# Weight sums of a Strassen product moved from GpSimd beside the projections to VectorE beside the first MLP product

## The chip, the cores and the metric

The kernel runs on one core of a Trainium2 chip. The metric is the device time of one execution in microseconds (us). TensorE (PE) multiplies, VectorE (DVE) and GpSimd (POOL) do elementwise work, ScalarE (ACT) evaluates functions and copies, and SyncE (SP) issues nearly all DMAs in one in-order queue. SBUF is the memory on the chip that the engines read; PSUM holds the products.

## The reference, cut to what matters

One decoder layer on 2048 tokens of width 1024 in float32: RMS norm, one input projection, three mixers (a causal convolution with 31 taps, retention, dilated attention), an output projection with residual, and an MLP with hidden width 4096:

```
h2 = rms_norm(x, norm2_g)
ff = square(relu(h2 @ w_ff1)) @ w_ff2
return x + ff
```

The change concerns sums of blocks of `w_ff2`. They depend on that input alone, so they can be made at any time before the second MLP product uses them.

## The kernel before, in words

Every float32 product is made as three matmuls on rounded high and low halves (`hi*hi + hi*lo + lo*hi`). ACT writes the high half (L634) and DVE subtracts it from the raw value to get the low half (L636).

The stages, in order of time: the projections of the convolution and retention parts, with the retention recurrence and the convolution taps between them (to about 440 us); the projections of the attention part with what is left of the taps (to about 685 us); attention (to about 950 us); the output projection (to about 1168 us); then the MLP for each half H of the tokens (1024 each): the first product (H = 0: 1168 to 1489 us; H = 1: 1788 to about 2108 us) and the second one (H = 0: 1489 to 1788 us; H = 1: from 2108 us).

**The MLP** uses Strassen's scheme with seven block products for eight. In the first product a loop over 16 pairs of hidden blocks (`pair(j)`, L1106) makes seven products of twelve matmuls each. Weight sums S1 to S4 of `w_ff1` are made by POOL (`weight_sums`, L1097). A product's stationary operand comes from `op_a` (L1074): ACT copy and DVE subtraction into one of six buffers (`wcp`). Several products accumulate in the same PSUM bank, and DVE reads the bank between two of them (L1114, L1118, L1121 to L1125), so the later product waits for that read. The results go to the DRAM tiles `hid_d`. The second product (L1193) runs through seven products of 16 steps each, and loads in every step one block of weights and one of activations. Its weights are blocks of `w_ff2` or, in the products S1 to S4, sums of them from the DRAM tiles `w2s_d`; the first of these is the third product.

**The sums of `w_ff2`** are made by `w2_sums(j)` (L175), 16 times: two loads of 512 KB (L179), four POOL additions or subtractions of 128x512 (L183), and two stores of 512 KB (L185). Twelve calls stand in the loop over token tiles of the first projections (L464), four in that of the attention projections (L612). Their tiles come from the pool `stage` with three buffers, which the weights of the projections (L112), the bias bands and the attention operands also use. POOL does other small work of the same stages that others wait for: the reciprocal roots (`rsqrt`, L83), the gate products of the retention (L340, L407) and the low halves for attention (L589, L591).

**The order.** The context is opened with `schedule_with_timeline_sim=True` (L1297): the order of the instructions in each engine's queue is chosen when the program is built, on a simulated timeline, with the program's order as the preference. At run time each queue is strictly in order. `load_acc` (L1160) loads the eight residual tiles `acc` for the second product; it is attached to step 6 of the first product (L1190). The pool `ur` has 24 buffers of 4 KB in each partition; while the first MLP product runs, 20 of them hold its right operands (B11, B21, B22, T2, T3), and the result tile `t12` rotates through the rest.

Of the kernel before, what the change touches and what calls it, by code (L numbers as in the profile page):

```python
# [9 lines left out]
F32 = mybir.dt.float32  # L10
# [3 lines left out]
ALU = mybir.AluOpType  # L14
# [4 lines left out]
P = 128  # L19
# [24 lines left out]
CH = 512  # L44
# [3 lines left out]
def kernel(ctx, tc, x, xT, w_in, g1, g2, conv_w, conv_b, conv_g, ret_g, qk_g,  # L48
                             w_out, w_ff1, w_ff2, rel_bias, ident_c, bands_c, rope_c, decay_c,
                             causal_c, groups_c, sel_c, outT):  # L50
    nc = tc.nc
# [11 lines left out]
    NP = NF // 2  # L63
    hid_d = [[[dram.tile([P, 2, CH], F32, name=f"hid_d{h}_{j}_{n}") for n in range(3)] +
              [dram.tile([P, 1, CH], F32, name=f"hid_d{h}_{j}_3")] for j in range(NP)] for h in range(2)]
    w2s_d = [[dram.tile([P, 2, CH], F32, name=f"w2s_d{j}_{n}") for n in range(2)] for j in range(NP)]
# [23 lines left out]
    stage = ctx.enter_context(tc.tile_pool(name="stage", bufs=3))  # L90
# [71 lines left out]
    def bias_bands(b):  # L162
        bands = stage.tile([33, TW], F32, tag="raw", name="bands")
        nc.sync.dma_start(out=bands[:], in_=bands_c[:, b, :])
        for h0 in range(0, HEADS, 2):
            bt = stage.tile([P, 2, TW], F32, tag="raw", name="bt")
            for u in range(2):
                pb = psA.tile([P, 512], F32, tag="c", name="pb", bufs=1)
                nc.tensor.matmul(pb[:, :TW], rb[:, h0 + u:h0 + u + 1].to_broadcast([33, P]), bands[:],
                                 start=True, stop=True)  # L170
                nc.scalar.activation(out=bt[:, u, :], in_=pb[:, :TW], func=AF.Copy)
            for u in range(2):
                nc.sync.dma_start(out=band_d[(h0 + u) * 3 + b].rearrange("(q w) -> q w", w=TW), in_=bt[:, u, :])

    def w2_sums(j):  # L175
        ra, rb = [stage.tile([P, 2, 512], F32, tag="raw", name=n) for n in ("w2sa", "w2sb")]
        for u, t in enumerate((ra, rb)):
            f = 2 * j + u
            nc.sync.dma_start(out=t[:], in_=w_ff2[f * P:(f + 1) * P, :].rearrange("p (h c) -> p h c", h=2))  # L179
        for out, a, b, op in ((rb[:, 1], ra[:, 1], rb[:, 1], ALU.add), (ra[:, 1], ra[:, 0], ra[:, 1], ALU.subtract),  # L180
                              (ra[:, 0], rb[:, 1], ra[:, 0], ALU.subtract),
                              (rb[:, 0], rb[:, 0], ra[:, 0], ALU.subtract)):
            nc.gpsimd.tensor_tensor(out=out, in0=a, in1=b, op=op)  # L183
        for u, t in enumerate((ra, rb)):
            nc.sync.dma_start(out=w2s_d[j][u][:], in_=t[:])  # L185


    x_first = [load_x(0, 4)]
# [2 lines left out]
    def prefetch(i, n=KT):  # L191
        hq[i] = split_x(x_first.pop(0) if x_first else load_x(i), n)
# [13 lines left out]
    rb = cv1.tile([33, HEADS], F32, name="rb")  # L206
# [227 lines left out]
    def go(g, taps=0):  # L434
        next(g, None)
        some_conv(taps)
# [14 lines left out]
    for i in range(2, NT - 2):  # L451
        c, r, b = conv_of[i], ret_of[i], ret_of[i - 1]
        go(c, 1)
        go(b, 1)
        if i == 2:
            go(ret_of[0])
        go(r, 1)
        go(b, 1)
        go(c, 1)
        prefetch(i + 1)  # L460
        go(r, 1)
        if 4 <= i < 7:
            bias_bands(i - 4)
        w2_sums(i - 2)  # L464
        go(r, 0)
        go(b, 0)
        go(r, 0)
# [107 lines left out]
    def load_tables(p):  # L575
        return [band_table(p, b, b < 2) for b in range(3)]

    def build(p, c, wait=0):
        cs = slice(c * CH, (c + 1) * CH)
        for h in range(2):  # L580
            raw = stage.tile([P, 2, CH], F32, tag="raw", name="qkraw")
            for u in range(2):
                nc.sync.dma_start(out=raw[u * 64:(u + 1) * 64], in_=qkT_d[p][c][h * 64:(h + 1) * 64])

            def parts(h=h, raw=raw):
                with tc.issue_after(last[0].ins):
                    nc.vector.tensor_copy(out=qs[h][:, cs], in_=raw[:, 0, :])
                    nc.vector.tensor_copy(out=khi[h][:, cs], in_=raw[:, 1, :])
                nc.gpsimd.tensor_tensor(out=qs[h][64:P, cs], in0=raw[64:P, 0, :],  # L589
                                        in1=qs[h][64:P, cs].bitcast(F32), op=ALU.subtract)  # L590
                nc.gpsimd.tensor_tensor(out=klo[h][:, cs], in0=raw[:, 1, :], in1=khi[h][:, cs].bitcast(F32),  # L591
                                        op=ALU.subtract)

            if wait:
                todo.append([wait, parts])
            else:
                parts()

    go(att_of[0])
    for i in range(2, NT):  # L600
        go(att_of[i], 1)
        go(att_of[i - 1])
        if i + 1 < NT:
            prefetch(i + 1)
        go(att_of[i], 1)
        go(att_of[i])
        if i % 4 == 1 and i > 4:
            build(0, i // 4 - 1)
        if i == 8:
            tabs = load_tables(0)  # L610
        if i % 2 == 0 and i <= 8:
            w2_sums(NP - 5 + i // 2)  # L612
    go(att_of[NT - 1])
    some_conv(100)
    second.close()
# [278 lines left out]
    def bank(name):  # L894
        turn[0] += 1
        tag = ("mm", "s", "pt", "o", "mm", "s", "pt", "c")[turn[0] % 8]
        return psA.tile([P, CH], F32, tag=tag, name=name, bufs=1 if tag in "oc" else 2)
# [27 lines left out]
    ur = ctx.enter_context(tc.tile_pool(name="ur", bufs=UNITS, side="right", reuse_waits="tile"))  # L925
# [19 lines left out]
    def tt(eng, out, a, b, op):  # L945
        eng.tensor_tensor(out=out, in0=a, in1=b, op=op)  # L946
# [53 lines left out]
    def right_ops(H, names):  # L1000
        for name, h, c in (("T3", 0, 1), ("T1", 0, 0), ("T4", 4, 0), ("B22", 4, 1)):
            if name in names:
                for kp in range(4):
                    op_b(name, kp, x1[H, kp + h][:, c, :])
# [59 lines left out]
                               5: [lambda: right_ops(0, ("T3", "T1"))]})  # L1064
    right_ops(0, ("T4", "B22"))

    for H in range(2):

        def load_w1(f):
# [36 lines left out]
        def pair(j, begun=None, loaded=None):  # L1106
            if not loaded:
                ra, rb = load_w1(2 * j), load_w1(2 * j + 1)
                loaded = ra, rb, weight_sums(ra, rb)
            ra, rb, (s12, s34) = loaded  # L1110
            dt, et, xb = begun or first_half(ra)
            yb = bank("psy")
            product(yb[:], op_a("S2", s12[:, 1, :]), "T2", True, True)
            tt(nc.vector, dt[:, 1, :], et[:, 0, :], yb[:], ALU.add)  # L1114
            if not begun:
                second_half(ra, dt, xb)
            product(yb[:], op_a("S3", s34[:, 0, :]), "T3", False, True)
            tt(nc.vector, et[:, 1, :], et[:, 0, :], yb[:], ALU.add)  # L1118
            zb = bank("psz")
            product(zb[:], op_a("S1", s12[:, 0, :]), "T1", True, True)  # L1120
            tt(nc.vector, et[:, 1, :], et[:, 1, :], zb[:], ALU.add)  # L1121
            product(yb[:], op_a("A22", rb[:, 1, :]), "T4", False, True)
            tt(nc.vector, et[:, 0, :], et[:, 0, :], yb[:], ALU.add)
            product(zb[:], op_a("S4", s34[:, 1, :]), "B22", False, True)
            tt(nc.vector, dt[:, 1, :], dt[:, 1, :], zb[:], ALU.add)  # L1125
            for t in (et[:], dt[:, 1, :]):
                nc.scalar.activation(out=t, in_=t, func=AF.Relu)
            for t in (et, dt):
                nc.scalar.activation(out=t[:], in_=t[:], func=AF.Square)
            t12 = unit4(ur, "u", "t12", F32)  # L1130
            nc.sync.dma_start(out=hid_d[H][j][1][:], in_=et[:])
            tt(nc.vector, t12[:, 0, :], dt[:, 1, :], dt[:, 0, :], ALU.subtract)
            tt(nc.vector, t12[:, 1, :], et[:, 1, :], t12[:, 0, :], ALU.subtract)
            tt(nc.vector, dt[:, 1, :], et[:, 1, :], dt[:, 1, :], ALU.subtract)
            nc.sync.dma_start(out=hid_d[H][j][0][:], in_=dt[:])
            nc.sync.dma_start(out=hid_d[H][j][2][:], in_=t12[:])
            tt(nc.vector, et[:, 0, :], et[:, 0, :], t12[:, 1, :], ALU.subtract)
            nc.sync.dma_start(out=hid_d[H][j][3][:], in_=et[:, 0:1, :])

        begun = []  # L1140
        ra, rb = load_w1(0), load_w1(1)
        loaded = ra, rb, weight_sums(ra, rb)
        begun.append(first_half(ra))
        for j in range(1, FIRST):
# [3 lines left out]
            ra = rj  # L1148
# [34 lines left out]
        def left_next():  # L1183
            for kp in range(4):
                for name, k in (("B11", kp), ("B21", kp + 4)):
                    op_b(name, kp, x1[1, k][:, 0, :])

        steps = {} if H else {(3, 8): load_next, (4, 2): lambda: normalise(1, 0), (4, 8): lambda: normalise(1, 1),
                              (5, 6): left_next, **{(6, 9 + kp): lambda kp=kp: act_sums(1, kp) for kp in range(4)}}
        steps[0, 6] = load_acc  # L1190
        sb = banks(("mm", "mm", "s", "s"))
        zb = banks(("pt", "pt", "o", "c"))
        for n, (an, bn, chain, dh, c, done) in enumerate((  # L1193
# [7 lines left out]
            for j in range(NP):  # L1201
                pool, tag = (stage, "raw") if n == 0 and j < 7 else (ur, "u")
                raw = pool.tile([P, 2, CH], F32, tag=tag, name="ffraw")
# [9 lines left out]
            for d in range(4):  # L1213
                t = acc[dh + d][:, c, :]
# [86 lines left out]
```

## Time and profile before

| what | value |
|---|---|
| median of 3 runs | 2416.18 us (2404.49 to 2425.15) |
| the profiled execution, its own time | 2412.23 us |
| its span, first to last instruction | 2410.1 us |
| PE busy | 2340.6 us (97%) |
| DVE busy | 1529.0 us (63%) |
| ACT busy | 1100.7 us (46%) |
| POOL busy | 592.4 us (25%) |
| mean granted TensorE clock | 0.981 |

Busy shares are means over stages. PE's time lies in the stretches where it idles or where its granted clock is below 1, and both are in the stages before the MLP. A wait is put down to the event that came last; the line of a helper (L636, L946) stands for all its uses, which the tile names tell apart.

### The profile page before, as it was taken

Reading aid. Unit: us, or ns where it says so; the run is one execution under the profiler, and the core shown is the slowest. Engines: PE = TensorE matmul, PEld = TensorE weight load, DVE = VectorE, ACT = ScalarE, POOL = GpSimd, SP = SyncE. Lnnn points to the kernel's source line nnn. Section 1 sums busy time; section 2 is a strip of 40 time slices with the busy share of each in tenths; the row PEclk is TensorE's granted clock in tenths of the full one; section 3 lists DMA queues with packets and bytes.
Section 4 is the critical chain, followed back from the end, with each engine's and each line's share of the span. In section 5 each row is a group of like instructions: output and inputs, shape, how many; then the busy total and the mean of one; then the engine's idle time right before and its main releaser. Section 6 shows DMA issues by size and latency. Waiting matters only on the chain.

```text
span 2410.1 us, 33394 instructions
## 1 busy us (share of the span) xinstructions
PE 2340.6 (97%) x11678; PEld 1957.3 (81%) x11678; DVE 1529.0 (63%) x2944; ACT 1100.7 (46%) x2309; POOL 592.4 (25%) x427
## 2 busy tenths in 40 slices
PE   7999999998999999899999999999999999999999
PEld 7878788898987777687888888888887888888887
DVE  5496979685348676568565555676576555565554
ACT  6443223533357667444444444545444444454442
POOL 1332661534213242334422330000022322000000
PEclk9999999999989899999999999999999999999999
DMA  7532552644245353855344447974624444698640
GB/s 239 167 116 91 164 181 60 187 122 141 77 99 109 80 115 87 288 184 178 109 166 153 145 144 273 379 260 123 205 101 144 144 145 146 213 381 286 194 146 35
DMA packets 256532, 396.45 MB, mean 164 GB/s; under 512 B 47485, under 2 KB 136684, under 8 KB 256364
## 3 DMA queue, kind: packets, MB, share of 16 engines
q1 hardware_dynamic: 253804, 385.93, 49.1%
q0 software_dynamic: 2560, 8.39, 0.9%
q8 instruction: 92, 1.51, 0.3%
q14 instruction: 76, 0.62, 0.1%
HBM read 280.30 MB, written 113.93 MB: 164 GB/s over the span
## 4 chain that ended last, share of the span: by engine, by line
PE 76%; DVE 11%; DMA 7%; POOL 2%; issue 2%; ACT 1%; SPq 1%; ACTq 0%; POOLq 0%; DVEq 0%
PE pso L934 25%; PE psy L934 11%; PE ps L160 10%; PE psx L934 7%; PE psz L934 7%; DVE acc L231 4%; PE psc L934 4%; PE po L729 2%; PE pt L708 2%; PE sp L682 2%; PE sp L683 2%; DMA xn<-x 2%; DMA ml_d<-ml 1%; DMA qkraw<-qkT_d 1%; DMA woraw<-w_out 1%
## 5 line engine op out<-in xcount | busy, mean ns | idle before, releaser
L934 PE MATMUL pso<-hid,w 128*128 128x512 f32 x2688 | 610.2, 389 | 0.0
L934 PEld LDWEIGHTS pso<-hid,w 128*128 128x128 f32 x2688 | 504.5, 188 | 105.1 <-ACT hid L634 0.2
L160 PE MATMUL ps<-whi,hh 128*128 128x384 f32 (+1 forms) x896 | 316.4, 354 | 14.8 <-ACT whi L119 9.5
L160 PE MATMUL ps<-whi,hl 128*128 128x384 f32 (+1 forms) x896 | 316.6, 353 | 0.5 <-DVE hl L152 0.5
L160 PE MATMUL ps<-wlo,hh 128*128 128x384 f32 (+1 forms) x896 | 314.4, 351 | 0.0
L634 ACT ACTIVATE w<-ffraw 128x512 fp32r<-128x512 f32 x224 | 141.5, 632 | 310.0 <-PE pso L934 273.9
L636 DVE TENSOR_TENSOR w<-ffraw,w 128x512 fp32r<-128x512 f32 x224 | 155.9, 696 | 196.6 <-ACT w L634 195.7
L946 POOL TENSOR_TENSOR s<-w1raw 128x512 f32<-128x512 f32 x64 | 85.2, 1351 | 712.8 <-PE pso L934 322.2
L934 PE MATMUL psy<-T,S 128*128 128x512 f32 x768 | 194.4, 395 | 0.0
L160 PEld LDWEIGHTS ps<-whi,hh 128*128 128x128 f32 x896 | 170.9, 191 | 28.4 <-ACT whi L119 9.5
L231 DVE SCALAR_TENSOR_TENSOR acc<-cbuf,cwt,acc 128x512 f32<-128x512 f32 x240 | 192.1, 849 | 0.2
L934 PE MATMUL psx<-B,A 128*128 128x512 f32 x768 | 189.7, 395 | 0.0
L160 PEld LDWEIGHTS ps<-whi,hl 128*128 128x128 f32 x896 | 171.1, 191 | 10.1 <-issue 2.7
L160 PEld LDWEIGHTS ps<-wlo,hh 128*128 128x128 f32 x896 | 171.1, 191 | 9.5 <-issue 2.7
L934 PEld LDWEIGHTS psx<-B,A 128*128 128x128 f32 x768 | 143.9, 187 | 35.1
L934 PEld LDWEIGHTS psy<-T,S 128*128 128x128 f32 x768 | 143.8, 187 | 34.7
L934 PE MATMUL psc<-mix,wohi 128*128 128x512 f32 x512 | 165.3, 403 | 6.1 <-ACT wohi L658 3.9
L636 DVE TENSOR_TENSOR hid<-ffraw,hid 128x512 fp32r<-128x512 f32 x224 | 152.7, 685 | 6.2 <-ACT hid L634 4.9
L636 DVE TENSOR_TENSOR S<-s,S 128x512 fp32r<-128x512 f32 x128 | 112.5, 883 | 58.2 <-ACT S L634 57.7
L693 ACT ACTIVATE lt<-lt,ml 128x256 f32<-128x256 f32 (+1 forms) x288 | 129.2, 452 | 28.9 <-DVE ml L690 28.2
L634 ACT ACTIVATE hid<-ffraw 128x512 fp32r<-128x512 f32 x224 | 137.2, 618 | 6.7 <-DMA ffraw<-hid_d 6.4
L634 ACT ACTIVATE A<-w1raw 128x512 fp32r<-128x512 f32 x96 | 60.1, 628 | 170.6 <-PE psy L934 126.7
(196 smaller groups left out, 3997.2 us busy)
## 6 DMA issues: line engine op xcount, KB each, us to landing
ffraw<-hid_d SPq DMA_DIRECT2D x224, 256.0 KB, 5.2
w1raw<-w_ff SPq DMA_DIRECT2D x66, 512.0 KB, 3.6
ffraw<-w2s_d SPq DMA_DIRECT2D x128, 256.0 KB, 4.0
ffraw<-w_ff SPq DMA_DIRECT2D x96, 256.0 KB, 5.3
woraw<-w_out SPq DMA_DIRECT2D x33, 512.0 KB, 4.3
hid_d<-hidB SPq DMA_DIRECT2D x32, 512.0 KB, 3.6
hid_d<-t SPq DMA_DIRECT2D x32, 512.0 KB, 2.6
hid_d<-hidA SPq DMA_DIRECT2D x32, 512.0 KB, 3.3
```

What stands on the lines that cost most here:

```text
L160: nc.tensor.matmul(ps, a[:, k, :], b[k][:], start=(k == 0 and m == 0), stop=(k == KT - 1 and m == 2))
L231: nc.vector.scalar_tensor_tensor(out=accs[j], in0=src, scalar=cwt[:, j, w:w + 1], in1=accs[j], op0=ALU.mult, op1=ALU.add)
L634: nc.scalar.activation(out=u[:, 0, :], in_=raw, func=AF.Copy)
L636: sub.tensor_tensor(out=u[:, 1, :], in0=raw, in1=u[:, 0, :].bitcast(F32), op=ALU.subtract)
L682: nc.tensor.matmul(sp[:, c0:c0 + n], qs[h][:, qsl], khi[h][:, ksl], start=True, stop=False)
L683: nc.tensor.matmul(sp[:, c0:c0 + n], qs[h][:, qsl], klo[h][:, ksl], start=False, stop=True)
L693: last_exp[0] = nc.scalar.activation(out=lt[:, :n], in_=lt[:, :n], func=AF.Exp, scale=-1.0, bias=mls[u][:, h:h + 1], accum_out=mls[u][:, 2 ...
L708: nc.tensor.transpose(pts[u][:, q * P:(q + 1) * P], lts[h, u][:, c * P:(c + 1) * P], ident[:])
L729: nc.tensor.matmul(po[h * 64:(h + 1) * 64, u0 * P:(u0 + n) * P], vt[:, kv, h * 64:(h + 1) * 64], mv, start=(one or i == 0), stop=(one or i ...
L934: nc.tensor.matmul(ps, w[a], act[b], start=(first and m == 0), stop=(last and m == 2), skip_group_check=more)
L946: eng.tensor_tensor(out=out, in0=a, in1=b, op=op)
```

## The change

`w2_sums` moves into the MLP: it is called from `pair(j)` in the first half (H = 0), after the DVE read of the bank that follows product S3. The calls are spread over j = 1 to 13, one sum each, and two at j = 4, 8 and 12. Its tiles come from `ur`, and the four operations run on DVE. The calls in both projection loops are gone. `load_acc` goes from step 6 to step 9 of the first of the seven products, in both halves.

```
-        w2_sums(i - 2)
...
-        if i % 2 == 0 and i <= 8:
-            w2_sums(NP - 5 + i // 2)
...
+    def w2_sums(j):
+        ra, rb = [ur.tile([P, 2, CH], F32, tag="u", name=n) for n in ("w2sa", "w2sb")]
+        for u, t in enumerate((ra, rb)):
+            f = 2 * j + u
+            nc.sync.dma_start(out=t[:], in_=w_ff2[f * P:(f + 1) * P, :].rearrange("p (h c) -> p h c", h=2))
+        for out, a, b, op in ((rb[:, 1], ra[:, 1], rb[:, 1], ALU.add), (ra[:, 1], ra[:, 0], ra[:, 1], ALU.subtract),
+                              (ra[:, 0], rb[:, 1], ra[:, 0], ALU.subtract),
+                              (rb[:, 0], rb[:, 0], ra[:, 0], ALU.subtract)):
+            tt(nc.vector, out, a, b, op)
+        for u, t in enumerate((ra, rb)):
+            nc.sync.dma_start(out=w2s_d[j][u][:], in_=t[:])
...
             tt(nc.vector, et[:, 1, :], et[:, 0, :], yb[:], ALU.add)
+            if H == 0 and 0 < j < 14:
+                for n in range(j - 1 + (j > 4) + (j > 8) + (j > 12), j + (j >= 4) + (j >= 8) + (j >= 12)):
+                    w2_sums(n)
...
-        steps[0, 6] = load_acc
+        steps[0, 9] = load_acc
```

## Rows read from the trace of the kernel before

**Rows 1.** Windows: length, busy PE, PEld, DVE, ACT, POOL (instructions), PEclk, DMA share, GB/s.

```profile
60.00:80.00 20.00, 18.57 (x113) 16.06 (x112) 10.78 (x30) 5.25 (x11) 11.63 (x12) 0.86 0.53 171
...
240.00:280.00 40.00, 36.90 (x214) 31.61 (x213) 36.60 (x59) 10.37 (x27) 21.81 (x11) 0.99 0.50 163
280.00:320.00 40.00, 35.55 (x169) 30.21 (x168) 33.71 (x49) 9.47 (x24) 27.98 (x17) 0.84 0.50 165
...
360.00:400.00 40.00, 38.33 (x220) 32.94 (x220) 37.20 (x77) 9.76 (x25) 8.05 (x6) 1.00 0.10 29
...
520.00:560.00 40.00, 33.54 (x186) 33.22 (x185) 35.15 (x42) 10.86 (x19) 23.31 (x14) 0.91 0.59 170
...
1300.00:1400.00 100.00, 100.00 (x432) 80.74 (x431) 57.88 (x82) 45.21 (x67) 27.64 (x20) 1.00 0.43 154
...
1489.00:1550.00 61.00, 61.00 (x270) 50.33 (x269) 38.91 (x61) 33.57 (x56) 0.00 (x0) 1.00 1.03 386
```

**Rows 2.** Windows of line L183 (the sums) alone: POOL busy, clock, DMA.

```profile
240.00:360.00 120.00, 50.30 (x32) 0.94 0.52 173
...
sum 485.00, POOL 97.66; mean POOL 19.53
```

**Rows 3.** Waits in the first 700 us: who waited for whom, us, times, longest.

```profile
PE rpo L379 <- DVE rsm L365: 4.5, 2, 3.7
PE ps L160 <- ACT rv L329: 3.0, 1, 3.0
PE ptq L536 <- DVE raw L526: 10.1, 4, 6.5
ACT rsq L395 <- DVE st L390: 33.0, 10, 12.3
DVE qs L587 <- DMA qkraw<-qkT_d: 13.5, 4, 4.6
POOL w2sb L183 <- DMA w2sb<-w_ff: 34.3, 9, 7.0
SPq L185 <- POOL w2sa L183: 45.4, 14, 6.7
```

**Rows 4.** DVE's convolution taps (L231), by group, from 240, 480 and 526 us.

```profile
L231 DVE SCALAR_TENSOR_TENSOR acc<-cbuf,cwt,acc 128x512 f32<-128x512 f32 x46 | 40.7, 934 | 0.0
...
L231 DVE SCALAR_TENSOR_TENSOR acc<-cbuf,cwt,acc 128x512 f32<-128x512 f32 x38 | 26.7, 745 | 0.1
...
L231 DVE SCALAR_TENSOR_TENSOR acc<-cbuf,cwt,acc 128x512 f32<-128x512 f32 x22 | 23.0, 1078 | 0.1
```

**Rows 5.** Groups of the whole run: DVE on two SBUF inputs in the MLP.

```profile
L946 DVE TENSOR_TENSOR t<-hidA 128x512 f32<-128x512 f32 x32 | 22.2, 692 | 13.7 <-ACT hidA L1129 13.6
```

**Rows 6.** Timeline of one pair, DVE: start, length, instruction, idle before it.

```profile
1302.34 0.69 DVE L946 TENSOR_TENSOR hidB<-hidB,psy 128x512 f32<-128x512 f32 x1 [1.44 <-PE psy L934]
1303.01 0.69 DVE L636 TENSOR_TENSOR S<-s,S 128x512 fp32r<-128x512 f32 x1
...
1306.29 1.69 DVE L636 TENSOR_TENSOR S<-s,S 128x512 fp32r<-128x512 f32 x1 [2.00 <-ACT S L634]
...
1321.85 0.69 DVE L946 TENSOR_TENSOR hidB<-hidB,psy 128x512 f32<-128x512 f32 x1 [1.45 <-PE psy L934]
```

**Rows 7.** Timeline of the same pair: PE, then POOL.

```profile
1307.51 0.63 PE L934 MATMUL psy<-T,A 128*128 128x512 f32 x2
...
1304.89 2.54 POOL L946 TENSOR_TENSOR s<-w1raw 128x512 f32<-128x512 f32 x2 [14.02 <-DMA w1raw<-w_ff]
```

**Rows 8.** SP's waits in the first MLP product of the first half.

```profile
SPq L1071 <- DVE A L636: 147.6, 27, 10.5
```

**Rows 9.** The tile acc from 1460 to 1560 us: durations min/median/max, first to last.

```profile
L1163 SPq DMA_DIRECT2D acc<-x_d x8: 320/320/400, 1473.3 to 1488.0; - x8
L946 DVE TENSOR_TENSOR acc<-acc,pso x4: 680/680/689, 1526.7 to 1529.7; 128x512 f32<-128x512 f32 x4
...
DMA to landing us min/median/max: 5.8/7.5/8.8
```

More of the change, by code (lines that the diff above doesn't have):

```diff
@@ L173, in bias_bands @@
                 nc.sync.dma_start(out=band_d[(h0 + u) * 3 + b].rearrange("(q w) -> q w", w=TW), in_=bt[:, u, :])
[L175 to L185, printed above, removed]
     x_first = [load_x(0, 4)]
```

## The prediction

> **What bounds the kernel now.** I read the windows by stage first, to find where TensorE loses time at all. In the first product of the MLP's first half, where the sums are to go, PE is busy 100.00 of 100 us at clock 1.00, and likewise in the second product behind it [rows 1]. Nothing can be won there; the question is only whether the new work makes PE wait. Before the attention PE does lose time. I count a window's loss as its idle time plus the clock's shortfall times its length (below 1.00 part of the window ran at 1.2 instead of 2.4 GHz). From 60 to 80 us that is 1.43 + 0.14 x 20 = 4.2 us; from 240 to 280, 3.10 + 0.4 = 3.5; from 280 to 320, 4.45 + 0.16 x 40 = 10.9; from 520 to 560, 6.46 + 0.09 x 40 = 10.1 [rows 1]. Together 28.7 us.
>
> Next, line L183 alone, to see whether the sums stand there. They take 97.66 us of POOL, and 50.30 of these lie between 240 and 360 us [rows 2]. Then the waits, to see who held PE: mostly DVE results that came late (3.7 us for `rsm`, 6.5 us for `raw`), or an ACT copy, itself behind an ACT square that waited 12.3 us for DVE [rows 3]. Last, why DVE is late: its queue is nearly full there (36.60, 33.71 and 35.15 of 40 us [rows 1]), and a convolution tap takes 745 ns where no sum runs, 934 ns from 240 us and 1078 ns from 526 us [rows 4]. So the sums on POOL slow DVE, DVE is late, PE stops and then runs for a while at the lower clock.
>
> **The parts, costed.**
> *Removed, 64 POOL operations beside the projections.* What they take from DVE, by the taps alone: 46 x (934 - 745) ns = 8.7 us in 240 to 320, and 22 x (1078 - 745) ns = 7.3 us in 526 to 562 [rows 4]. Against that stand PE's longest waits of 3.0 and 3.7 us in the one stretch and 6.5 in the other [rows 3], so most of them should close, and the low clock behind them. I don't take all. POOL's operations for the attention operands and the reciprocal roots stay and slow DVE too, and DVE's wait of up to 4.6 us for `qkraw` [rows 3] has nothing to do with the sums. Of the 14.4 us between 240 and 320 I take 10, of the 10.1 behind 520 I take 6. Both are choices nearer to the upper end (all of it) than to the lower one (nothing, if another late result takes the place). From 60 to 80 us one sum is in the way early: POOL waits for its loads up to 7.0 us [rows 3], and the roots queue behind. I take 3 of the 4.2 us. Sum 19 us; bounds 0 and 28.7.
>
> *Removed, 64 DMAs and their places in SP's queue.* SP waited 45.4 us in L185 for POOL [rows 3], with loads of `x` and weights behind it. This is part of the same stalls, so it is not counted again; what hides it is PE's work queued ahead.
>
> *Added, 64 DVE operations in the first product.* The nearest row is DVE on two SBUF tiles of the same shape, 692 ns [rows 5]: 64 x 0.692 = 44 us. A pair takes 1321.85 - 1302.34 = 19.5 us [rows 6], and DVE is idle 42.12 of 100 us [rows 1], so 8.2 us a pair, against 4 x 0.692 = 2.8 us in ten pairs and 5.5 in three. On throughput it fits and costs nothing; if DVE were full, all 44 us would be paid.
>
> What can cost is order. DVE reads the bank after product S3 at 1302.34 to 1303.03 [rows 6], and the next product into that bank starts at 1307.51 [rows 7], a margin of 4.5 us. Four sums in front of such a read use 2.8 of it; a wait for their loads may use more. Behind that wait DVE's low halves and the other reads stand in queue, and PE waits for them. I take 2 us for the whole stage: two spare operand tiles per sum can be loaded well before DVE reaches it, because four of the 24 `ur` buffers are free of operands. Bounds 0 and the slow rival's price.
>
> Beside POOL a DVE operation of this kind takes 1.69 instead of 0.69 us [rows 6], one each pair. The Trainium skill (SBUF — State Buffer, "Who interferes with whom") says that a DVE instruction with two SBUF inputs and a GpSimd instruction that reads SBUF exclude each other, and that the one issued second blocks. The row agrees, and the rule speaks against the new place as well as the old one, since POOL makes the other weight sums there. Were each of the 64 to meet one such block of 1.0 us (the row's difference), they would take 108 us in place of 44; DVE's idle time in 13 pairs is 13 x 8.2 = 107 us. So by the rule at its worst DVE would be just full in these pairs, and at its best nothing changes in the sum.
>
> *Added, 64 DMAs in the first product.* A sum moves 4 x 0.52 MB = 2.1 MB in a pair, 108 GB/s on top of 154 [rows 1], twice that in the three double pairs: 262 and 370 GB/s. The second product runs at 386 GB/s with PE never idle [rows 1], so bandwidth is free. In SP's queue they are 4 x 0.32 us a pair (the length of an issue [rows 9]), where SP stands 147.6 us waiting at the `w_ff1` loads anyway [rows 8]. A store that waits for DVE holds these loads back. POOL starts at the moment its load lands, after 14.02 us of idleness [rows 7], so such a delay passes on to the sums S1 to S4, but their operands are made several products ahead. I put 0, bounded by the slow rival.
>
> *Moved, `load_acc` by three steps.* The eight loads start between 1473.3 and 1488.0 us and land after at most 8.8; the first use is at 1526.7 [rows 9]. The margin is 1526.7 - 1496.8 = 29.9 us. From the first load to the first use are 53 us, and no more than the product's sixteen steps lie in them, so three steps are about 10 us. It costs nothing, in both halves.
>
> **Sum:** 19 - 2 = 17 us less than the profiled execution's 2412.2 gives 2395. The median of the runs is 4 us above that execution, so on the median's scale it is 2399; I say 2398.
>
> **Rivals.**
> *All stalls close.* The 28.7 us go, and also the idle 1.67 us from 360 to 400, where DVE is busy 37.20 of 40 [rows 1]: 30 us, 2386 on the median's scale, or a little less if more of the low clock goes. For it: in each stretch the slowed DVE time is larger than PE's longest wait. Against: the same taps must still be done by DVE there, and the queue order is chosen anew, so that every earlier end may be spent on another wait.
>
> *The stalls are filled again.* Without the sums the next late thing holds PE: DVE's taps or `qkraw`. Then 0 to 8 us are won, 2408 to 2416. For it: DVE is at 84 to 92% of these windows, and without the taps' slowing still at (36.60 + 33.71 - 8.7) / 80 = 77% and (35.15 - 7.3) / 40 = 70% [rows 1, 4]. Against: PE was idle there only in short pieces, which the slowed operations cover.
>
> *Slower: DVE waits for the sums' loads.* On POOL the first operation waited for its load in 9 of 16 sums, 34.3 us in all, 3.8 on average [rows 3]. The same on DVE in front of a bank read passes the margin: 2.8 + 3.8 - 4.5 = 2.1 us of PE idleness each, 19 us for nine; with 7.0 us in all sixteen, 16 x 5.3 = 85 us. Taking 40, less the 17 won, the time is about 2439. It decides as soon as a wait exceeds 1.7 us at the wrong place. For it: the call stands right behind a bank read, and one queue orders all of DVE. Against: the loads need nothing but a free buffer, and in the old place three `stage` buffers were shared with the projection weights.
>
> **How the numbers follow.** Forecast 45%, all stalls close 22%, filled again 20%, slower 13%. About 1% (24 us) is what a measurement can tell from no change, so faster means below 2392. The forecast's own bounds (2385 to 2408) reach below that with about 9 of its 45%, which with the 22% makes faster 0.31 in all. Slower by over 1% (above 2440) is more than half of the slow rival, 0.08; the rest, 0.61, is no change. The range leaves out the far ends of the two outer cases: 2379 to 2425.
>
> **What would show it.** PE's idle time and clock loss between 240 and 320 us and between 520 and 560 us fall to some 4 us each; taps there take near 745 ns; the wait of PE for `raw` shrinks. In the first product of the first half PE stays busy in every microsecond at 19.5 us a pair, and DVE rises from 58 to about 72%. The forecast is wrong if PE waits for DVE in that product, or if the projections end no earlier than now because new waits stand where the old ones were.

## The result, and the profile after

The changed kernel takes 2384.44 us (median of 4 runs, 2382.88 to 2392.27) against 2419.41 for the kernel before (4 runs). The ratio is 0.9865, with a 95% interval of 0.9835 to 0.9896: faster by 1.0 to 1.7%. The medians are 35 us apart. The profiled executions differ by 2412.23 - 2384.19 = 28.0 us, and the time is accounted on those two. They are one execution each: over all series the kernel before ran from 2404 to 2433 us, so a few microseconds of such an account are not firm.

Where the 28 us come from is seen from the first and last start of one stage's matmuls. This is the view by tile of the changed kernel (duration minimum, median and maximum in ns, then first and last start in us): the last transposes of the attention projections, the output projection, and the first MLP product of the first half alone.

```profile
L523 PE MATMUL ptq<-ident,raw x96: 270/272/330, 453.6 to 656.8; 128*128 128x128 f32 x96
...
L919 PE MATMUL psc<-mix,wohi x512: 387/393/793, 922.4 to 1139.0; 128*128 128x512 f32 x171
...
L919 PE MATMUL psx<-B,A x384: 392/396/476, 1139.4 to 1443.0; 128*128 128x512 f32 x192
```

The same starts in the kernel before are 473.8 and 683.9, 948.4, and 1168.5 to 1471.9. So the projections end 683.9 - 656.8 = 27.1 us earlier. Attention takes 265.6 in place of 264.5 us, and the output projection 217.0 in place of 220.1. The first MLP product, which now holds the sums, spans 303.6 us in place of 303.4. The last PE instruction starts 27.5 us earlier, so the projections hold nearly all of it.

The windows of the changed kernel that answer to [rows 1] (columns as there; what comes after the earlier stalls has moved, so the line from 500 to 540 answers to 520 to 560):

```profile
60.00:80.00 20.00, 20.00 (x135) 17.61 (x134) 9.07 (x37) 9.33 (x24) 5.52 (x7) 1.00 0.49 144
80.00:100.00 20.00, 17.79 (x91) 14.47 (x89) 6.01 (x19) 10.21 (x25) 5.68 (x7) 1.00 0.52 159
240.00:280.00 40.00, 40.00 (x221) 35.24 (x220) 35.60 (x68) 11.71 (x28) 14.02 (x6) 1.00 0.21 59
280.00:320.00 40.00, 40.00 (x265) 34.59 (x264) 24.14 (x57) 13.97 (x38) 6.64 (x5) 1.00 0.13 40
500.00:540.00 40.00, 38.76 (x231) 38.40 (x230) 30.77 (x50) 14.26 (x25) 13.67 (x7) 1.00 0.44 111
1240.00:1340.00 100.00, 100.00 (x433) 80.76 (x431) 77.83 (x110) 46.61 (x67) 31.21 (x22) 1.00 0.79 288
1340.00:1440.00 100.00, 100.00 (x432) 80.73 (x431) 72.16 (x103) 48.16 (x70) 27.96 (x19) 1.00 0.72 258
```

PE neither idles nor loses clock between 240 and 320 us, where it had lost 14.4; of the 10.1 us lost from 520 to 560, 1.2 are left. A smaller loss appears at 80 to 100 us (2.2 us idle). In the first MLP product PE is busy in all of 200 us at clock 1.00, while DVE rises from 58 to 72 and 78%, and the DMA rate to 258 and 288 GB/s.

The taps of the changed kernel, by line, in two stretches that begin at 240 and at 526 us (busy us and mean ns of one behind the bar), answering to [rows 3, 4]:

```profile
L219 DVE SCALAR_TENSOR_TENSOR acc<-cbuf,cwt,acc 128x512 f32<-128x512 f32 x46 | 34.4, 793 | 0.0
...
L219 DVE SCALAR_TENSOR_TENSOR acc<-cbuf,cwt,acc 128x512 f32<-128x512 f32 x6 | 4.5, 748 | 0.1
```

And its waits: PE's for `raw`, then DVE's for the loads of the sums in their new place (who waited for whom, us, times, longest).

```profile
PE ptq L523 <- DVE raw L513: 4.2, 3, 2.4
...
DVE w2sb L931 <- DMA w2sb<-w_ff: 12.2, 8, 2.2
```

The last row is the slow rival's event: DVE does wait for the loads, in 8 of 16 sums and up to 2.2 us. No PE wait stands against it in that stage. The timeline shows why: here is DVE in one such pair.

```profile
1228.94 0.68 DVE L931 TENSOR_TENSOR hidB<-hidB,t 128x512 f32<-128x512 f32 x1
1231.61 0.69 DVE L931 TENSOR_TENSOR w2sb<-w2sa,w2sb 128x512 f32<-128x512 f32 x1 [1.99 <-DMA w2sb<-w_ff]
1232.22 0.69 DVE L621 TENSOR_TENSOR S<-s,S 128x512 fp32r<-128x512 f32 x1
1232.82 0.69 DVE L931 TENSOR_TENSOR w2sa<-w2sa 128x512 f32<-128x512 f32 x1
1233.54 0.69 DVE L931 TENSOR_TENSOR w2sa<-w2sb,w2sa 128x512 f32<-128x512 f32 x1
1234.27 0.69 DVE L931 TENSOR_TENSOR w2sb<-w2sb,w2sa 128x512 f32<-128x512 f32 x1
1234.88 0.68 DVE L931 TENSOR_TENSOR hidB<-hidB,psy 128x512 f32<-128x512 f32 x1
```

The sum stands ahead of a bank read, at 1234.88. Its wait of 1.99 us falls there too, one other operation (L621) stands among its four, and the read still comes in time for PE.

### The profile page after: what moved, and what is told of

Same layout as the page of the kernel before. It is cut to its first block, busy times and chain, and to the rows that moved or that the text cites. A ratio compares the mean times of both kernels' runs of the same rounds, so it can differ in the third digit from the quotient of the medians.

```text
span 2382.4 us, 33367 instructions
## 1 busy us (share of the span) xinstructions
PE 2328.6 (98%) x11678; PEld 1948.2 (82%) x11678; DVE 1522.4 (64%) x3008; ACT 1101.2 (46%) x2309; POOL 502.1 (21%) x363
## 4 chain that ended last, share of the span: by engine, by line
PE 86%; DMA 6%; DVE 4%; ACT 2%; issue 1%; POOL 1%; SPq 1%; ACTq 0%; DVEq 0%; POOLq 0%
PE pso L919 26%; PE ps L160 16%; PE psy L919 11%; PE psx L919 8%; PE psz L919 7%; PE psc L919 6%; DMA xn<-x 2%; PE po L714 2%; PE pt L693 2%; PE sp L667 2%; PE sp L668 2%; PE rsp L352 1%; DMA qkraw<-qkT_d 1%; DMA ml_d<-ml 1%; PE rpo L367 1%
## 5 line engine op out<-in xcount | busy, mean ns | idle before, releaser
L621 DVE TENSOR_TENSOR w<-ffraw,w 128x512 fp32r<-128x512 f32 x224 | 156.0, 697 | 198.7 <-ACT w L619 197.9
L931 POOL TENSOR_TENSOR s<-w1raw 128x512 f32<-128x512 f32 x64 | 90.1, 1428 | 710.3 <-PE pso L919 320.2
L219 DVE SCALAR_TENSOR_TENSOR acc<-cbuf,cwt,acc 128x512 f32<-128x512 f32 x240 | 175.6, 778 | 0.2
L621 DVE TENSOR_TENSOR hid<-ffraw,hid 128x512 fp32r<-128x512 f32 x224 | 152.9, 686 | 8.0 <-ACT hid L619 7.9
L619 ACT ACTIVATE hid<-ffraw 128x512 fp32r<-128x512 f32 x224 | 137.1, 617 | 16.6 <-DMA ffraw<-hid_d 14.4
L621 DVE TENSOR_TENSOR S<-s,S 128x512 fp32r<-128x512 f32 x128 | 107.0, 839 | 43.6 <-ACT S L619 42.9
```

Of the source, the lines that this page charges most:

```text
L219: nc.vector.scalar_tensor_tensor(out=accs[j], in0=src, scalar=cwt[:, j, w:w + 1], in1=accs[j], op0=ALU.mult, op1=ALU.add)
L619: nc.scalar.activation(out=u[:, 0, :], in_=raw, func=AF.Copy)
L621: sub.tensor_tensor(out=u[:, 1, :], in0=raw, in1=u[:, 0, :].bitcast(F32), op=ALU.subtract)
```

## The experiments

Two theories stood at the start. Theory 1, that of the prediction: POOL's operations slow DVE, DVE is late, PE stops. Theory 2: the transfers, with their places in SP's queue and in the three `stage` buffers, are what is late. "Projections end" below is the last start of the `ptq` matmuls, by the same view as above: 683.9 before, 656.8 after. The changed kernel and its five variants (e1, e2, e6, e8, e13) end the projections between 651.6 and 656.8 us, so differences under some 5 us are not read. Each such end is that of one profiled execution; the ratios are over all runs, and all are to the kernel before. The changed kernel's gain is 0.0135 of the time before, and "kept" below is the part of it that a variant does not win.

**e1: no sums at all.** From the changed kernel:

```
-            if H == 0 and 0 < j < 14:
-                ...
...
-            if name in ("A11", "A12", "A22"):
+            if name in ("A11", "A12", "A22") or name[0] == "S":
```

> The changed kernel with the sums left out altogether; the second MLP product reads plain blocks of w_ff2 in their place, in the same number and size (so the result is not the layer's). If the sums are hidden in the first MLP product, as forecast, this is no faster than the changed kernel: 2382 to 2386 us, and PE's gaps stay. If the sums there still cost DVE waits that reach PE, it is 5 to 20 us faster than the changed kernel (2365 to 2380).

2389.59 us, ratio 0.9849 (0.9829 to 0.987); the profiled execution spans 2382.3 us against 2382.4. The median is above the 2382 to 2386 expected, but so is that of the kernel before in the same series (2426.1 us), and the ratio is that of the changed kernel. The sums cost nothing that can be measured in their new place, and the gain is what their removal from the projections is worth.

**e4: the transfers alone beside the projections.** From the kernel before (the loop around the operation goes too):

```
...
-            nc.gpsimd.tensor_tensor(out=out, in0=a, in1=b, op=op)
```

> The kernel before without the 64 POOL operations; the 64 transfers stay beside the projections and store plain weights (so the result is not the layer's). Theory 1, POOL operations slow DVE and hold up POOL's queue: nearly the whole gain comes, 2384 to 2394 us, and the taps fall to about 750 ns. Theory 2, the transfers and their places in SP's queue and the three stage buffers are what is late: no more than a third comes, 2405 to 2416.

2392.24 us, ratio 0.9854 (0.9828 to 0.9879); projections end 655.6. All of the gain, with all 64 transfers still there. The taps fall to 780 ns from 40 to 565 us, not quite to the 750 expected. Between 240 and 320 us PE loses nothing, though the DMA engines are busier than in the kernel before:

```profile
240.00:280.00 40.00, 40.00 (x227) 36.01 (x226) 35.04 (x68) 11.14 (x27) 13.65 (x6) 1.00 0.95 317
280.00:320.00 40.00, 40.00 (x264) 34.62 (x263) 22.64 (x55) 14.20 (x39) 6.43 (x5) 1.00 0.52 182
```

Theory 2 falls: without the POOL operations the transfers cost nothing that can be measured. The run does not tell the operations' length from their waiting for loads, since both are gone.

**e5: the POOL operations alone.** From the kernel before:

```
...
-            nc.gpsimd.tensor_tensor(out=out, in0=a, in1=b, op=op)
...
+        for _ in range(4):
+            nc.gpsimd.tensor_tensor(out=scr[:], in0=scr[:], in1=scr[:], op=ALU.subtract)
```

> The kernel before without the 64 transfers; the POOL operations stay, on a scratch tile that is filled once, and the second product reads plain blocks of w_ff2 (so the result is not the layer's). Theory 1: DVE is still slowed, little is won, 2402 to 2416 us. Theory 2: 2384 to 2396. If both this and the run with transfers only are near 2385, it is the coupling of the two (POOL's queue waiting for a load) that costs.

2404.82 us, ratio 0.9909 (0.9888 to 0.9931); projections end 670.7. Not what was asked: with nothing to wait for, the planner put all 64 between 1.3 and 134.7 us, ahead of the stretches in question. A third of the loss is kept all the same: from 0 to 140 us, where the operations now stand, PE loses 12 us more than in the changed kernel (idle time and clock shortfall). e11 repeats it nearer to the old place.

**e2: the sums on POOL, in the new place.** From the changed kernel:

```
-            tt(nc.vector, out, a, b, op)
+            tt(nc.gpsimd, out, a, b, op)
```

> The changed kernel with the four operations of each sum on POOL, in the new place. If place alone matters, the same time as the changed kernel, 2382 to 2390 us: POOL is busy about 88 of 321 us there and gets about 90 more. If the engine matters (POOL's queue waits for loads in front of the weight sums S1 to S4 of w_ff1, or DVE is slowed too much), 2395 us or more, with PE waiting for ACT or DVE in the first MLP product.

2385.28 us, ratio 0.9838 (0.9808 to 0.9868). POOL's queue waits for the loads even longer than it did beside the projections, and PE waits for nobody in that stage:

```profile
POOL w2sb L931 <- DMA w2sb<-w_ff: 62.9, 9, 13.4
```

So in the new place the choice of engine makes no difference that can be measured; the place is enough.

**e3: the sums on DVE, in the old place.** From the kernel before:

```
-            nc.gpsimd.tensor_tensor(out=out, in0=a, in1=b, op=op)
+            nc.vector.tensor_tensor(out=out, in0=a, in1=b, op=op)
```

> The kernel before with the four operations of each sum on DVE, still beside the projections. If POOL as the engine was the fault, most of the gain comes, below 0.990. If the place is the fault, because DVE's queue is nearly full there (33 to 37 of 40 us) and now gets 44 us of work and the waits for the loads, nothing is won or it is slower: 0.998 to 1.012, with PE waiting for DVE.

2390.13 us, ratio 0.9892 (0.985 to 0.9934); projections end 668.4. The first branch came, "POOL as the engine was the fault", and my expectation for a full DVE was wrong: with 44 us more work on the busiest helper engine the projections still end 15.5 us earlier, of 27.1 with the sums gone from there; by the ratios four fifths of the gain come, and the two intervals overlap. So in the old place the move from POOL to DVE alone wins most of it. DVE's waits for the loads are short:

```profile
DVE w2sb L183 <- DMA w2sb<-w_ff: 10.7, 6, 3.8
```

A full DVE queue is thus not the fault by itself. That left two shares within the POOL operations: their length, shared with DVE, and what they wait for at the head of POOL's queue.

**e9: short POOL operations, all waits kept.** From the kernel before:

```
-            nc.gpsimd.tensor_tensor(out=out, in0=a, in1=b, op=op)
+            nc.gpsimd.tensor_tensor(out=out[:, 0:8], in0=a[:, 0:8], in1=b[:, 0:8], op=op)
```

> The kernel before with the 64 POOL operations cut to 8 of their 512 columns; loads, stores and waits stay (so the sums are incomplete and the result is not the layer's). The run with transfers only won the whole 1.5%, so the cost is in the POOL operations. Theory 1a, their length (DVE shares with them, and POOL's small operations stand behind them): nearly all of the gain again, 0.985 to 0.988 of the time before. Theory 1b, POOL's queue waits for the loads in front of the roots: about half of it or less, 0.992 to 1.000.

2414.92 us, ratio 0.9986 (0.9964 to 1.0009); projections end 678.4 in the profiled execution, the fastest of ten (2405.96 us). Nearly nothing is won, although the taps are as fast as after (777 ns from 40 to 565 us, 778 in the changed kernel, 849 in the kernel before). PE now waits for POOL: first PE's wait, then POOL's timeline at that place.

```profile
PE ptr L411 <- POOL ro L407: 19.7, 2, 14.2
```

```profile
281.34 0.20 POOL L183 TENSOR_TENSOR w2sb<-w2sa,w2sb 128x8 f32<-128x8 f32 x1 [4.85 <-DMA mix_d<-rm]
...
288.53 0.20 POOL L183 TENSOR_TENSOR w2sb<-w2sa,w2sb 128x8 f32<-128x8 f32 x1 [6.15 <-DMA w2sb<-w_ff]
...
289.53 1.32 POOL L83 TENSOR_TENSOR rrr<-rss,power 128x6 f32<-128x6 f32 x1
295.79 0.56 POOL L183 TENSOR_TENSOR w2sb<-w2sa,w2sb 128x8 f32<-128x8 f32 x1 [4.95 <-DMA w2sb<-w_ff]
...
299.75 1.44 POOL L407 TENSOR_TENSOR ro<-ro,rg 128x384 f32<-128x384 f32 x1
```

Three sums stand in POOL's queue ahead of `ro` and wait 4.85, 6.15 and 4.95 us for transfers (the profile puts the first wait down to a transfer to `mix_d`). The retention result `ro`, which PE needs, comes behind the last of them, and PE stands for 14.2 us.

**e12: no stores.** From the kernel before:

```
-        for u, t in enumerate((ra, rb)):
-            nc.sync.dma_start(out=w2s_d[j][u][:], in_=t[:])
...
```

> The kernel before without the 32 stores of the sums; loads and POOL operations stay (the second product reads plain blocks, so the result is not the layer's). A stage buffer is then free 2 to 3 us earlier and SP no longer stands in L185 for POOL. If the chain store, free buffer, load is what holds POOL's queue, a good part of the gain comes, 0.988 to 0.994, and POOL's waits for the loads fall below 20 us. If the POOL operations cost by themselves, 0.996 to 1.000.

2416.9 us, ratio 0.9976 (0.9957 to 0.9995); projections end 688.3, later than before. The waits that the profile puts down to `w2sb` loads did fall (14.2 us in 6), but POOL's idle time in front of the sums as a whole did not (80.8 us against 72.7 before), and PE waited 16.3 us for `ro`, longest 10.7. The stores are not a necessary link: SP's next loads now wait for the buffer that POOL frees, 42.3 us in 4 waits from 200 to 320 us, and POOL's queue is held up without the stores as well.

**e11: full POOL operations in place, no transfers.** From the kernel before (the input is the low halves that the step has just made):

```
-    def w2_sums(j):
...
+    def w2_sums(j, h):
...
+            nc.gpsimd.tensor_tensor(out=scr[:], in0=h[:, 4 * (k % 2):4 * (k % 2) + 4, :] ..., in1=scr[:], op=ALU.subtract)
```

> The kernel before with the 64 POOL operations kept at full size beside the projections, each reading the low halves of the token tile that its step prepares, but without the 64 transfers (the second product reads plain blocks of w_ff2, so the result is not the layer's). It asks whether full POOL operations cost without loads to wait for. If sharing between POOL and DVE costs the time by itself: 0.993 or more of the time before, with taps over 820 ns. If the cost needs the chain store, free buffer, load in front of POOL's queue: 0.985 to 0.990.

2407.03 us, ratio 0.9934 (0.9911 to 0.9956); projections end 674.4. The ratio lies at the edge of the first branch, and its interval reaches below. About half of the loss is kept; in the profiled pair it is 674.4 - 656.8 = 18 us of 27. The taps are as slow as in the kernel before (856 ns against 849; their line is L227 here), and PE stands for DVE's `raw` (6.1 us at longest) as it did before. The operations are not free of waits: POOL waits for DVE's low halves in front of them, 52.8 us in 11, and its other work still stands behind them. So the run shows what full operations cost without waits for loads; it does not tell their sharing with DVE from their standing in front of POOL's other work. First the taps by line, then the wait:

```profile
L227 DVE SCALAR_TENSOR_TENSOR acc<-cbuf,cwt,acc 128x512 f32<-128x512 f32 x240 | 194.5, 856 | 0.2
```

```profile
PE ptq L532 <- DVE raw L522: 8.6, 3, 6.1
```

By the ratios e11 keeps about half of the loss, e12 eight tenths and e9 nine tenths, so length and waits for loads cost less together than their sum.

Where each of them loses tells more. These are PE's losses by stretch, idle time and clock shortfall counted as in the prediction, from windows of 20 us:

| us of each run | before | changed | e11, no loads | e9, short | e12, no stores |
|---|---|---|---|---|---|
| 60 to 140 | 6.9 | 2.3 | 12.2 | 1.9 | 0.9 |
| 140 to 240 | 0.0 | 0.0 | 2.2 | 7.3 | 8.7 |
| 240 to 340 | 14.5 | 0.0 | 1.0 | 22.6 | 25.4 |
| 500 to 580 | 10.7 | 1.9 | 10.1 | 2.4 | 10.0 |

The windows of the two old stalls, first in e11, then in e9:

```profile
280.00:320.00 40.00, 38.99 (x224) 34.41 (x223) 35.63 (x62) 12.59 (x30) 19.39 (x14) 1.00 0.12 34
520.00:560.00 40.00, 33.87 (x186) 33.55 (x186) 31.76 (x43) 11.28 (x19) 17.16 (x10) 0.91 0.23 68
```

```profile
280.00:320.00 40.00, 25.83 (x142) 22.85 (x140) 20.25 (x39) 7.10 (x21) 10.59 (x23) 0.79 0.81 287
520.00:560.00 40.00, 37.63 (x224) 37.02 (x223) 32.17 (x49) 12.98 (x24) 15.28 (x14) 1.00 0.73 214
```

The later stall is there in the three runs with full POOL operations beside that stretch (before, e11, e12), each time with a wait for `raw` of 5.9 to 6.5 us, and gone with short ones (e9, 1.7 us): it goes with the operations' length. The earlier stall is there in the three runs in which the sums wait for loads (before, e9, e12) and gone in e11, though its taps from 240 to 320 us take 885 ns. Slow taps alone did not make that one, with the reserve that e11 has somewhat less POOL work there (26.1 us of such operations between 240 and 320 against 33.5). The kernel before has the load in the chain of work that ended last from 262 to 312 us: four of its pieces, from the load to DVE's use of the root behind the sum.

```profile
276.06 5.12 DMA w2sb<-w_ff
...
281.31 1.56 POOL w2sb L183
282.87 2.49 POOL rrr L83
...
285.38 1.26 DVE rrr L402
```

**e8 and e13: more work on DVE in the new place.** From the changed kernel, every operation of a sum twice (e8), or the first two of the four (e13):

```
-            tt(nc.vector, out, a, b, op)
+            for _ in range(2):
+                tt(nc.vector, out, a, b, op)
```

> The changed kernel with each of the 64 DVE operations issued twice (so the sums and the result are not the layer's): 88 us of DVE in place of 44 in the first MLP product. By throughput it still fits (about 8.2 us idle in each of 13 pairs, 107 us) and the time stays that of the changed kernel, 0.984 to 0.988. By the margin of 4.5 us at the bank reads, eight operations in a row (5.5 us) pass it in each pair, and PE waits for DVE there: 10 us or more above the changed kernel, 0.990 to 1.000.

e8: 2422.77 us, ratio 1.0016 (0.9992 to 1.0041), more than either branch expected; the first MLP product spans 342.5 us in place of 303.6. The windows of its middle 200 us:

```profile
1240.00:1340.00 100.00, 88.41 (x360) 69.06 (x359) 85.56 (x117) 35.32 (x53) 26.47 (x16) 0.97 0.67 244
1340.00:1440.00 100.00, 93.98 (x385) 73.88 (x385) 89.34 (x118) 40.59 (x60) 32.65 (x20) 0.97 0.66 241
```

and PE's wait for DVE in that stage:

```profile
PE psy L919 <- DVE hidA L931: 14.8, 7, 3.6
```

Over 100 us DVE is not full (86 and 89%), and still PE idles and loses clock, waiting at the accumulating bank `psy` for DVE's read. That is the place which the slow rival named. But no eight operations in a row stand ahead of the read. These are the 10 us before the longest such wait (3.59 us) and before another of 2.26 us, then DVE's timeline in the second:

```profile
1246.64:1256.64 10.00, 6.41 (x28) 4.88 (x26) 10.00 (x12) 3.77 (x5) 6.66 (x4) 1.00 0.34 120
1315.16:1325.16 10.00, 7.74 (x35) 5.94 (x33) 9.48 (x10) 3.98 (x5) 6.34 (x4) 1.00 0.34 115
```

```profile
1317.00 1.78 DVE L931 TENSOR_TENSOR w2sa<-w2sb,w2sa 128x512 f32<-128x512 f32 x1
1318.82 1.67 DVE L931 TENSOR_TENSOR w2sb<-w2sb,w2sa 128x512 f32<-128x512 f32 x1
1320.40 0.68 DVE L931 TENSOR_TENSOR hidB<-hidB,psy 128x512 f32<-128x512 f32 x1
```

DVE is full there for 10 us, 9.48 to 10.00 before each of the seven waits on `hidA`, with other work between the sums' operations. Some of these take 1.7 to 1.8 us, while POOL makes the weight sums of `w_ff1`: the 128 operations sum to 118 us of DVE, not the 88 that 0.69 us each would give.

> The changed kernel with the first two of each sum's four DVE operations issued twice, six in all (so the result is not the layer's): 66 us of DVE. Eight operations cost 39 us in the first MLP product, four cost nothing. Six in a row take 4.1 us, just under the margin of 4.5 us at a bank read: if that margin decides, 0 to 8 us above the changed kernel, 0.985 to 0.990. If the cost grows evenly from four operations on, some 19 us, 0.993 to 0.996.

e13: 2390.38 us, ratio 0.9873 (0.9841 to 0.9905); the first MLP product spans 308.8 us. Four operations cost 0.2 us there, six 5, eight 39, each from one profiled execution. The margin's branch came in time. That the margin decides is not shown: e13's operations, too, were slowed beside POOL (80 us in place of 66).

**e6: `load_acc` at step 6.** From the changed kernel:

```
-        steps[0, 9] = load_acc
+        steps[0, 6] = load_acc
```

> The changed kernel with load_acc back at step 6. If its place has some 20 us of margin either way, the same time, 0.984 to 0.988, and PE's short wait of 1.2 us at the start of the second product may go or stay. If the later loads had cost or saved something, more than 3 us off the changed kernel.

2380.19 us, ratio 0.986 (0.9817 to 0.9903). No difference, as the margin in [rows 9] said.

## Why the prediction was right, and where its size was off

Direction and place held; the mechanism is shown for one of the two large stalls. The measured 2384.44 us lies in the stated range, but just below the forecast's own bounds (2385 to 2408): it is in because the range was widened for the rivals. The forecast was a gain of 17 us; the profiled pair shows 28.0 and the medians 35. The rival "all stalls close", 2386 us at 22%, is what happened, and by the prediction's limit of 2392 us the result is "faster", to which it gave 0.31 against 0.61 for no change. Point by point:

- **The removed POOL operations: 19 us taken, 27.1 measured.** This is the mis-sized term (27.1 us is how much earlier the projections end). I took 3, 10 and 6 us of the three stretches and expected some 4 us to stay in each of the later two; 0 and 1.2 us stayed. I had withheld part because POOL's other operations and the `qkraw` wait would keep DVE late. They remain in the changed kernel and in e4, and PE lost nothing by them between 240 and 320 us.
- **The reason given was half of it.** The prediction named the slowing of DVE. e11 bears it out for the stall behind 520 us. For the one from 240 us it does not: there slow taps without waits for loads cost 1.0 us, and e9, with fast taps, loses more than the kernel before by POOL's queue, where a sum that waits for its load stands ahead of `ro`. The rows had POOL's waits [rows 3], and I used them only for the first stretch. Since either part alone keeps half of the loss or more, the slowed taps were no measure of what removal would bring; the stalls' own length was.
- **The removed transfers: nothing, right.** e4 keeps them all and is as fast.
- **The added DVE work: 2 us taken, 0.2 measured.** Hidden, as e1 shows. With more work PE waits at the bank reads, as the margin argument says (e8). But DVE is full in the 10 us before each of the seven waits on `hidA`, so a local lack of DVE time is the rival, and no run tells the two apart.
- **Blocks of 1.0 us beside POOL: nearly none, with four operations.** In the new place a sum's four operations take 690 to 752 ns on average, against 692 in [rows 5], some 2 us in all. With eight (e8) the operations take 30 us more than at 692 ns each, so the case that the prediction held up as the worst is part of what came there.
- **`load_acc`: nothing, right** (e6).
- **What the signs were to be.** PE busy throughout the first product: yes. DVE at 72% there: 72 and 78%. Taps near 745 ns: 748 from 526 us, but 793 from 240, and PE has no stall there all the same.

What stays open is how the loss before divides between the two parts. Every variant is also ordered anew by the planner, so its losses are costs of another order, not shares of one. In the earlier stall of the kernel before, PE's own waits were for `rsm` and for an ACT copy behind DVE [rows 3], not for `ro` as in e9 and e12, so there both parts may be at work.

## What to carry to other kernels

Work that can be done at any time should stand where one engine bounds and the others have room, and the room to count is what is free just ahead of the tightest hand-over, not the idle share of the stage: here four operations were free, six cost 5 us and eight 39, with the engine still idle a tenth of the time on average. In an in-order queue, ask of background work not only how long it takes but what it waits for, because that wait is inherited by whatever small operation stands behind it. Test the parts of such a cost one at a time and also together: either alone may keep half of it or more.

## What the runs showed that was not expected

A tiny POOL operation seems to be held for many DVE operations. In e9 one on 128x8 elements, 0.20 us long elsewhere, took 7.44 us while DVE issued taps and other operations on two SBUF tiles back to back, and it ended about when DVE turned to an operation that reads PSUM (`rsm`). The last of the same sum's four took 5.18 us and ended so too. POOL's view, then DVE's:

```profile
260.06 7.44 POOL L183 TENSOR_TENSOR w2sb<-w2sa,w2sb 128x8 f32<-128x8 f32 x1 [4.26 <-DMA w2sb<-w_ff]
267.58 0.20 POOL L183 TENSOR_TENSOR w2sa<-w2sa 128x8 f32<-128x8 f32 x1
```

```profile
261.06 4.05 DVE L231 SCALAR_TENSOR_TENSOR acc<-cbuf,cwt,acc 128x512 f32<-128x512 f32 x6
...
265.38 2.06 DVE L231 SCALAR_TENSOR_TENSOR acc<-cbuf,cwt,acc 128x512 f32<-128x512 f32 x3
267.37 0.67 DVE L365 TENSOR_TENSOR rsm<-rsp,causal 128x512 f32<-128x512 f32 x1
```

The Trainium skill (SBUF — State Buffer, "Who interferes with whom") calls the port pair that the two engines share an exclusive lock, and says that a VectorE instruction with two SBUF inputs contends with a GpSimd instruction that reads SBUF. The rows agree that POOL is kept waiting, and suggest that it can be for some ten DVE instructions in a row. No run here tested it; it is read from times that coincide, and durations on POOL are rough in this profile. If it holds, sharing works in both directions: POOL slows DVE (the taps, 778 to 849 ns), and DVE keeps POOL from its turn.
